# The opening of a transformer layer as one list of steps, with the order of ScalarE and VectorE fixed up to raw tile 25

## The chip, the core and the metric

The kernel runs on one core of a Trainium2 chip. TensorE (PE) multiplies and transposes, VectorE (DVE) and ScalarE (ACT) work element by element, GpSimd (POOL) does little here, and SyncE (SP) issues the loads from HBM to SBUF. Each engine works through its own queue in order. The metric is the time of one execution on the device in microseconds (us), less is better.

## The reference

One layer for 256 tokens of width 2048: a gated feed-forward block, a mixer of two attention branches, a second feed-forward block and a norm, each block conditioned on a vector c through nine vectors of modulation. The opening of the kernel computes the first lines of this:

```python
mod = (jax.nn.silu(c) @ w_ada[i] + b_ada[i]).reshape(B, N_MOD, D)
sh1, sc1, ga1, sh2, sc2, ga2, sh3, sc3, ga3 = [mod[:, j, None, :] for j in range(N_MOD)]
h = _rms_norm(x, g_ffn1[i]) * (1.0 + sc1) + sh1
x = x + 0.5 * ga1 * _swiglu(h, w1_a[i], w3_a[i], w2_a[i])
...
def _swiglu(h, w1, w3, w2):
    return (jax.nn.silu(h @ w1) * (h @ w3)) @ w2
```

All inputs are fp32. `w_ada` is 2048 by 18432, `w1_a` and `w3_a` are 2048 by 5632.

## The kernel before

Weights come in tiles of 128 partitions by 2048 fp32 numbers, 1 MiB each, called **raw tiles**. Almost all products are made in three passes (`mm3`): ScalarE casts half a raw tile at a time to the reduced type fp32r (`wh`, L125), VectorE subtracts to get the rest (`wl`, L126), and TensorE adds wh x hTh, wl x hTh and wh x hTl (L137, L140, L141). hTh and hTl are the two parts of the transposed, normed and modulated input h, by k-tile of 128 rows of the contraction.

The **opening** computes twelve results of the first feed-forward block (six chunks of 512 columns for `w1_a` and for `w3_a`), by 48 raw tiles of four weight blocks each. `opening_order` fixes which blocks a raw tile holds. The contraction runs in three groups of k-tiles: k-tile 0 alone (raw 0 to 2, in plain fp32, L630), k-tiles 1 to 5 (raw 3 to 17), k-tiles 6 to 15 (raw 18 to 47). A raw tile of the later groups is 24 products. Results that have ended in one group leave PSUM and are added up in SBUF (`add_up`): ScalarE copies the first part (L586), VectorE adds the later ones (L580).

A k-tile of h needs its modulation first, and that takes 32 **ada tiles**, two for each k-tile, numbered 0 to 31 here: VectorE multiplies each with silu(c) and sums along the row (L194). Then come two columns on ScalarE (`ab`, L528 and L530), hf (L542), hTh (two casts, L555) and hTl on VectorE (L562). x itself is scaled, transposed by TensorE and copied back in blocks of four k-tiles (L345, L348, L513).

Loads are all issued by SP, in the order of the program. A raw or ada tile takes a buffer from one of two pools, three buffers `raws` and a ring of seven shared with the sums in SBUF (`ramp_raw`); six sums leave one of the seven from raw 8 on. A load waits on SP until the last reader of its buffer has ended, and what is behind it waits too.

What sets the order before: the loop over raw tiles (`for r, grp in enumerate(raws_of)`, L656) loads ada tiles up to a target for each raw tile (`target`, L494), prepares h as soon as its ada tiles are known (`h_tiles`, `low_tiles`), splits the raw tile (`split_raw`) and records its products. TensorE's instructions of the first two groups and SP's loads are held in program order. Those of ScalarE and VectorE are placed by a scheduler, with a few hints (`issue_after`).

Of the kernel before, what the change touches and what calls it, by code (L numbers as in the profile page):

```python
# [63 lines left out]
def layer_kernel(ctx: ExitStack, tc: tile.TileContext, a: dict):
# [396 lines left out]
    with tc.tile_pool(name="f1", bufs=1, reuse_waits="tile") as f1, \  # L461
# [50 lines left out]
        def keep_x(tb, k0, ps):
            ACT.copy(x_sb[:, tb, k0 * P:(k0 + 4) * P], ps)  # L513
            for k in range(4):
                xnT.pop((k0 + k, tb))

        def h_tiles(known):

            while h_rows:
                k0, n = h_rows[0]  # L520
                if any((j, k) not in (known if n > 1 else ada_done) for j in range(2) for k in range(k0, k0 + n)):
                    return
                h_rows.pop(0)
                if k0 == 0:
                    mod_cols(0, 0, 1, C_GF1)
                for k in range(max(k0, 1), k0 + n):
                    with tc.issue_after(last_cast[0].ins) if n > 1 else nullcontext():
                        ACT.activation(ab[0][:, k:k + 1], mod[:, KT + k:KT + k + 1], AF.Identity,  # L528
                                       scale=cols[:, C_GF1 + k:C_GF1 + k + 1], bias=gbs[0][:, k:k + 1])
                        ACT.activation(ab[0][:, KT + k:KT + k + 1], mod[:, k:k + 1], AF.Identity,  # L530
                                       bias=cols[:, C_BADA + k:C_BADA + k + 1])
                hf = wkB("hf") if k0 else hl.tile([P, 1024], F32, tag="wh", name="hf")
                hf = hf[:, :TB * n * P].rearrange("p (t k n) -> p t k n", t=TB, k=n)
                for k in range(n):
                    scale, bias = ab[0][:, k0 + k:k0 + k + 1], ab[0][:, KT + k0 + k:KT + k0 + k + 1]
                    if (k0 + k, 0) in xnT:
                        for tb in range(TB):
                            with tc.issue_after(last_xn[0].ins):
                                first_hf[0] = ACT.activation(hf[:, tb, k], xnT[k0 + k, tb], AF.Identity, scale=scale, bias=bias)
                    else:  # L540
                        with tc.issue_after(last_cast[0].ins) if n > 1 else nullcontext():
                            ACT.activation(hf[:, :, k], x_sb[:, :, (k0 + k) * P:(k0 + k + 1) * P], AF.Identity,  # L542
                                           scale=scale, bias=bias)
                if k0 == 0:
                    gb = wk.tile([P, 16], F32, tag="gb", name="gb", bufs=1)
                    DVE.scalar_tensor_tensor(out=gb, in0=cols[:, C_BADA + KT:C_BADA + 2 * KT], scalar=1.0,
                                             in1=cols[:, C_GF1:C_GF1 + KT], op0=ALU.add, op1=ALU.mult)
                    gbs.append(gb)
# [891 lines left out]
```

## Time and profile before

| | |
|---|---|
| median of three runs | 2144.58 us (2140.0 to 2145.95) |
| the profiled execution | 2144.17 us |
| its span, first to last instruction | 2142.3 us |
| mean granted TensorE clock | 0.997 |
| loads over the span | 546.47 MB read, mean 256 GB/s |

The views used are: the page (busy time of each engine over the span); tables by window, in which each row is a stretch of the span with the busy us and number of instructions of each engine, the granted clock, the busy share of the DMA engines and GB/s; the waits, grouped by who waited for whom (total us, times, longest); and rows of the timeline (start us, duration us, engine, source line, operation, out<-in with shapes, number of instructions merged into the row, and in brackets the idle time before the row and what ended it).

### The profile page before, as it was taken

Reading aid. Unit: us, or ns where it says so; the run is one execution under the profiler, and the core shown is the slowest. Engines: PE = TensorE matmul, PEld = TensorE weight load, DVE = VectorE, ACT = ScalarE, POOL = GpSimd, SP = SyncE. Lnnn points to the kernel's source line nnn. Section 1 sums busy time; section 2 is a strip of 40 time slices with the busy share of each in tenths; the row PEclk is TensorE's granted clock in tenths of the full one; section 3 lists DMA queues with packets and bytes.
Section 4 is the critical chain, followed back from the end, with each engine's and each line's share of the span. In section 5 each row is a group of like instructions: output and inputs, shape, how many; then the busy total and the mean of one; then the engine's idle time right before and its main releaser. Section 6 shows DMA issues by size and latency. Waiting matters only on the chain.

```text
span 2142.3 us, 26049 instructions
## 1 busy us (share of the span) xinstructions
PE 2111.0 (99%) x10192; PEld 1757.9 (82%) x10192; DVE 1621.5 (76%) x1809; ACT 1045.5 (49%) x1320; POOL 41.7 (2%) x63
## 2 busy tenths in 40 slices
PE   8899999999999999999999999999999999999998
PEld 5677888888888879888877788778888888888886
DVE  5888667878777877565777778887688678857875
ACT  6546433343443465655544434475455445535553
POOL 0000000000000001010000000000000000000000
PEclk9999999999999999999999999999999999999999
DMA  9898668999988846445878788955555555555563
GB/s 394 325 372 329 241 237 325 352 338 337 351 332 306 324 153 210 163 165 198 301 289 302 277 332 302 338 204 194 202 194 191 205 177 196 215 197 196 178 216 118
DMA packets 79102, 550.30 MB, mean 257 GB/s; under 512 B 9409, under 2 KB 9969, under 8 KB 14082
## 3 DMA queue, kind: packets, MB, share of 16 engines
q1 hardware_dynamic: 76176, 542.06, 69.3%
q0 software_dynamic: 1344, 3.17, 0.5%
q10 hardware_dynamic: 1458, 3.40, 0.4%
q8 instruction: 80, 1.31, 0.2%
q14 instruction: 44, 0.36, 0.0%
HBM read 546.47 MB, written 2.12 MB: 256 GB/s over the span
## 4 chain that ended last, share of the span: by engine, by line
PE 85%; DVE 5%; DMA 5%; ACT 3%; issue 1%; POOL 0%; SPq 0%; POOLq 0%; ACTq 0%; DVEq 0%
PE a L137 9%; PE a L140 9%; PE a L141 9%; PE y L137 8%; PE y L140 8%; PE y L141 8%; PE pacc L140 3%; PE pacc L141 3%; PE pacc L137 3%; DVE wl L126 2%; DMA raw<-in_w_out 2%; ACT wh L125 2%; DVE raw L194 1%; DMA raw<-in_w_open 1%; PE qkv L137 1%
## 5 line engine op out<-in xcount | busy, mean ns | idle before, releaser
L125 ACT CAST wh<-raw 128x1024 fp32r<-128x1024 f32 (+2 forms) x678 | 690.9, 1040 | 860.4 <-DMA raw<-in_w_a 209.0
L126 DVE TENSOR_TENSOR wl<-raw,wh 128x1024 fp32r<-128x1024 f32 (+2 forms) x678 | 805.0, 1209 | 340.6 <-ACT wh L125 337.6
L194 DVE SCALAR_TENSOR_TENSOR raw<-raw,c_bc 128x2048 f32<-128x2048 f32 x144 | 329.2, 2287 | 26.8 <-DMA raw<-in_w_ada 25.7
L137 PE MATMUL a<-wh,hTh 128*128 128x512 f32 (+1 forms) x904 | 340.1, 376 | 0.1
L140 PE MATMUL a<-wl,hTh 128*128 128x512 f32 (+1 forms) x904 | 339.5, 376 | 0.0
L141 PE MATMUL a<-wh,hTl 128*128 128x512 f32 (+1 forms) x904 | 339.2, 375 | 0.0
L137 PE MATMUL y<-wh,gT 128*128 128x512 f32 x704 | 275.6, 391 | 0.2
L140 PE MATMUL y<-wl,gT 128*128 128x512 f32 x704 | 274.3, 390 | 0.0
L141 PE MATMUL y<-wh,gT 128*128 128x512 f32 x704 | 273.7, 389 | 0.0
L141 PEld LDWEIGHTS a<-wh,hTl 128*128 128x128 f32 x904 | 170.2, 188 | 31.0 <-DVE hTl L369 0.3
L137 PEld LDWEIGHTS a<-wh,hTh 128*128 128x128 f32 x904 | 170.3, 188 | 30.4 <-ACT wh L125 0.6
L140 PEld LDWEIGHTS a<-wl,hTh 128*128 128x128 f32 x904 | 170.3, 188 | 29.3
L137 PEld LDWEIGHTS y<-wh,gT 128*128 128x128 f32 x704 | 132.2, 188 | 29.6 <-ACT gT L392 1.8
L141 PEld LDWEIGHTS y<-wh,gT 128*128 128x128 f32 x704 | 132.1, 188 | 27.5
L140 PEld LDWEIGHTS y<-wl,gT 128*128 128x128 f32 x704 | 132.2, 188 | 27.0
L140 PE MATMUL pacc<-wl,hTh 128*128 128x512 f32 x360 | 141.9, 394 | 4.9 <-DVE wl L126 4.9
L137 PE MATMUL pacc<-wh,hTh 128*128 128x512 f32 x360 | 137.1, 394 | 7.2 <-ACT wh L125 6.3
L141 PE MATMUL pacc<-wh,hTl 128*128 128x512 f32 x360 | 140.6, 391 | 0.7 <-DVE hTl L562 0.7
L1272 DVE TENSOR_TENSOR wl<-right,wh 128x1024 fp32r<-128x1024 f32 x60 | 73.5, 1224 | 30.4 <-ACT wh L1271 29.9
L1271 ACT CAST wh<-right 128x1024 fp32r<-128x1024 f32 x60 | 63.2, 1053 | 56.0 <-PE m L141 24.8
L137 PEld LDWEIGHTS pacc<-wh,hTh 128*128 128x128 f32 x360 | 67.9, 189 | 24.0 <-ACT wh L125 8.4
L140 PEld LDWEIGHTS pacc<-wl,hTh 128*128 128x128 f32 x360 | 67.9, 189 | 21.8 <-DVE wl L126 8.1
(353 smaller groups left out, 3099.1 us busy)
## 6 DMA issues: line engine op xcount, KB each, us to landing
raw<-in_w_ada SPq DMA_DIRECT2D x144, 1024.0 KB, 5.9
raw<-in_w_b SPq DMA_DIRECT2D x102, 1024.0 KB, 4.8
raw<-in_w_a SPq DMA_DIRECT2D x84, 1024.0 KB, 5.5
raw<-in_w_in SPq DMA_DIRECT2D x60, 1024.0 KB, 5.0
raw<-in_w_open SPq DMA_DIRECT2D x45, 1024.0 KB, 6.3
raw<-in_w_s SPq DMA_DIRECT2D x30, 1024.0 KB, 4.8
raw<-in_w_out SPq DMA_DIRECT2D x16, 1024.0 KB, 6.4
raw<-in_w_proj_a SPq DMA_DIRECT2D x8, 1024.0 KB, 4.8
```

The costliest lines, as they stand in the source:

```text
L125: last_cast[0] = ACT.copy(wh[:, :w], src)
L126: DVE.tensor_tensor(wl[:, :w], src, wh[:, :w].bitcast(F32), op=ALU.subtract)
L137: m = PE.matmul(out, xh, wh, start=start, stop=False)
L140: PE.matmul(out, xh, wl, start=False, stop=False)
L141: PE.matmul(out, xl, wh, start=False, stop=stop)
L194: last_ada[0] = DVE.scalar_tensor_tensor(out=raw, in0=raw, scalar=1.0, in1=c_bc, op0=ALU.mult, op1=ALU.mult, accum_out=dst)
L1271: ACT.copy(wh[:, :n], src)
L1272: DVE.tensor_tensor(wl[:, :n], src, wh[:, :n].bitcast(F32), op=ALU.subtract)
```

## The change

The loop for raw tiles 0 to 25 is replaced by a list of steps, `opening_steps`, that a table of functions carries out one by one. Each letter is a step: A loads an ada tile, a multiplies it, R loads a raw tile, K and k make wh and wl of half of it, G makes the columns of a k-tile on ScalarE (g makes them on VectorE), H its hTh, h its hTl, F the first hf, X, T and Y scale, transpose and copy back a block of x, P records the products of one weight block, S opens a fourth accumulator, C and c move an ended sum on ScalarE or VectorE. Every instruction of these steps is held in program order (`pin`), on ScalarE and VectorE too. From raw tile 26 on the loop is as before. What is computed is the same; the columns of k-tiles 1 and 5 move from ScalarE to VectorE.

```diff
+BY_ROW = 26
...
+def opening_steps(order):
...
+    add("A A R0 A R1 A A R2 A R3")
+    add("Y F Y Y Y P0.0 X P0.1 T C H0.1 a h0.1 X C P0.2 T Y X P0.3 T C Y X")
+    add("P1.0 T C Y a g1.1 P1.1 C Y H1.1 a h1.1 S P1.2 C P1.3 C C P2.0 P2.1 P2.2 P2.3")
+    add("A R4 a K3.0 K3.1 k3.0 k3.1 G2.1 H2.1 P3.0 P3.1 P3.2 P3.3")
+    add("a h2.1 A A R5 K4.0 K4.1 k4.0 k4.1 a G3.1 H3.1 P4.0 P4.1 P4.2 P4.3")
+    add("A A R6 a h3.1 K5.0 K5.1 k5.0 k5.1 a G4.1 H4.1 P5.0 P5.1 P5.2 P5.3")
+    add("A R7 a K6.0 K6.1 k6.0 h4.1 k6.1 a g5.1 P6.0 P6.1 P6.2 P6.3")
+    add("R8 K7.0 H5.1 K7.1 k7.0 h5.1 k7.1 P7.0 P7.1 P7.2 P7.3")
+    loaded = done = 12
+    rows, low = list(range(6, KT, 2)), ""
+    for r in range(8, BY_ROW):
+        n = min(2 * KT, 12 + (20 * (r - 7) + 17) // 18) - loaded
+        add("A " * n + f"R{r + 1} K{r}.0 K{r}.1 k{r}.0 k{r}.1 {low} {ends(r - 1)}")
+        loaded += n
+        low = ""
+        if rows and 2 * rows[0] + 4 <= done:
+            add(f"G{rows[0]}.2 H{rows[0]}.2")
+            low = f"h{rows.pop(0)}.2"
+        add(f"P{r}.0 P{r}.1 P{r}.2 P{r}.3 " + "a " * (loaded - done))
+        done = loaded
+    add(low + " " + " ".join(f"G{k}.2 H{k}.2 h{k}.2" for k in rows))
+    return out
...
-        early = (2, 3, 5, 7, 8, 10, 11, 12)
-        marks = [(len(early) - 1, early[-1]), (25, n_ada), (len(raws_of), n_ada + ADA_END)]
...
+        def cast(r, q):
+            wh, wl = (hl.tile([P, 1024], F32R, tag=t, name=t) for t in ("wh", "wl"))
+            last_cast[0] = pin(ACT.copy(wh, raw_of[r][:, q * 1024:(q + 1) * 1024]))
+            part_of[r, q] = wh, wl
+
+        def cast_low(r, q):
+            wh, wl = part_of[r, q]
+            pin(DVE.tensor_tensor(wl, raw_of[r][:, q * 1024:(q + 1) * 1024], wh.bitcast(F32), op=ALU.subtract))
...
+        for s in script[2:]:
+            steps[s[0]](*s[1:])
...
-        for r, grp in enumerate(raws_of):
-            known = set(ada_done)
-            fill(int(target(r)) - (n_all - len(ada_q)))
...
+        for r in range(BY_ROW, len(raws_of)):
+            grp = raws_of[r]
```

Three places in the engines' queues. First SP, the loads behind raw 2. Names carry buffer numbers: before, raw_325, 374, 422 and 467 are raw 3 to 6; after, raw_228, 333, 381 and 426. Before:

```order
L665 DMA raw_301<-in_w_open 128x1024
L108 DMA raw_319<-in_w_ada 128x2048
L108 DMA raw_322<-in_w_ada 128x2048
L108 DMA raw_325<-in_w_open 128x2048
L108 DMA raw_371<-in_w_ada 128x2048
L108 DMA raw_374<-in_w_open 128x2048
L108 DMA raw_416<-in_w_ada 128x2048
L108 DMA raw_419<-in_w_ada 128x2048
L108 DMA raw_422<-in_w_open 128x2048
L108 DMA raw_464<-in_w_ada 128x2048
L108 DMA raw_467<-in_w_open 128x2048
```

After the change:

```order
L675 DMA raw_224<-in_w_open 128x1024
L150 DMA raw_226<-in_w_ada 128x2048
L150 DMA raw_228<-in_w_open 128x2048
L150 DMA raw_331<-in_w_ada 128x2048
L150 DMA raw_333<-in_w_open 128x2048
L150 DMA raw_377<-in_w_ada 128x2048
L150 DMA raw_379<-in_w_ada 128x2048
L150 DMA raw_381<-in_w_open 128x2048
L150 DMA raw_422<-in_w_ada 128x2048
L150 DMA raw_424<-in_w_ada 128x2048
L150 DMA raw_426<-in_w_open 128x2048
```

Raw 3, 4 and 5 have each moved ahead of one ada tile.

Second ScalarE, around the casts of raw 3 and raw 4 (wh from raw_325 and raw_374). Before:

```order
L528 ACTIVATE ab0_83<-mod_80,gb_216,small_77 128x1
L530 ACTIVATE ab0_83<-mod_80,small_77 128x1
L542 ACTIVATE hf_343<-x_sb_76,ab0_83 128x256
L555 CAST hTh_147<-hf_343 128x128
L555 CAST hTh_149<-hf_343 128x128
L528 ACTIVATE ab0_83<-mod_80,gb_216,small_77 128x1
L125 CAST wh_327<-raw_325 128x1024
L125 CAST wh_331<-raw_325 128x1024
L530 ACTIVATE ab0_83<-mod_80,small_77 128x1
L542 ACTIVATE hf_388<-x_sb_76,ab0_83 128x256
L125 CAST wh_376<-raw_374 128x1024
L125 CAST wh_380<-raw_374 128x1024
```

After, with raw_228 and raw_333:

```order
L607 COPY sum3_320<-pacc_95 128x1024
L680 CAST wh_336<-raw_228 128x1024
L680 CAST wh_339<-raw_228 128x1024
L565 ACTIVATE ab0_83<-mod_80,gb_164,small_77 128x1
L567 ACTIVATE ab0_83<-mod_80,small_77 128x1
L582 ACTIVATE hf_346<-x_sb_76,ab0_83 128x256
L586 CAST hTh_147<-hf_346 128x128
L586 CAST hTh_149<-hf_346 128x128
L680 CAST wh_383<-raw_333 128x1024
L680 CAST wh_386<-raw_333 128x1024
```

Before, columns and hf of k-tile 2 (hf_343) and the first column of k-tile 3 stand ahead of the casts of raw 3; after, the casts stand ahead of the columns and hf of k-tile 2 (hf_346).

Third SP again, later: raw_835, 875, 921 and 960 are raw 15 to 18 before, raw_806, 843, 889 and 930 after. Before:

```order
L108 DMA raw_835<-in_w_open 128x2048
L108 DMA raw_869<-in_w_ada 128x2048
L108 DMA raw_872<-in_w_ada 128x2048
L108 DMA raw_875<-in_w_open 128x2048
L108 DMA raw_918<-in_w_ada 128x2048
L108 DMA raw_921<-in_w_open 128x2048
L108 DMA raw_957<-in_w_ada 128x2048
L108 DMA raw_960<-in_w_open 128x2048
```

After:

```order
L150 DMA raw_806<-in_w_open 128x2048
L150 DMA raw_841<-in_w_ada 128x2048
L150 DMA raw_843<-in_w_open 128x2048
L150 DMA raw_887<-in_w_ada 128x2048
L150 DMA raw_889<-in_w_open 128x2048
L150 DMA raw_926<-in_w_ada 128x2048
L150 DMA raw_928<-in_w_ada 128x2048
L150 DMA raw_930<-in_w_open 128x2048
```

The two ada tiles in a row have moved from ahead of raw 16 to ahead of raw 18; the same goes for raw 25, which had two ahead of it and now has one.

More of the change, by code (lines that the diff above doesn't have):

```diff
@@ L60, in opening_order, with add, ends @@
     return [slots[q:q + 4] for q in range(0, len(slots), 4)]
+def opening_steps(order):
+    out = []
+    def add(text):
+        for t in text.split():
+            out.append((t[0],) + tuple(int(v) for v in t[1:].split(".") if v))
+    def ends(r):
+        return " ".join("c" if c < 4 else "C" for gi, c, wi, k in order[r]
+                        if gi == 1 and k == STARTS[2] - 1 and (c, wi) not in FRONT[2])
+    add("A A R0 A R1 A A R2 A R3")
[20 more added lines that the diff above has]
+    return out
 @with_exitstack
@@ L512, in keep_x @@
[L512 to L533, printed above, removed]
-                for k in range(n):
[L535 to L548, printed above, removed]
@@ new lines, in x_turn, with x_keep, ada_load @@
+                pin(PE.transpose(ps[:, k * P:(k + 1) * P], xn[:, k * P:(k + 1) * P], ident))
+            xbs.append((k0, tb, ps))
+            return ps
+        def x_keep():
+            k0, tb, ps = xbs.pop(0)
+            pin(ACT.copy(x_sb[:, tb, k0 * P:(k0 + 4) * P], ps))
+        ada_tiles = [(j, kt) for kt in range(KT) for j in (1, 0)]
+        ada_raws = []
+        def ada_load():
+            j, kt = ada_tiles.pop(0)
+            ada_raws.append((j, kt, load_unit(a["w_ada"][j, kt], pool=ramp_raw)))
@@ new lines, in ada_product, with columns @@
+        def ada_product():
+            j, kt, raw = ada_raws.pop(0)
+            ada_done.add((j, kt))
+            return pin(DVE.scalar_tensor_tensor(out=raw, in0=raw, scalar=1.0, in1=c_bc, op0=ALU.mult, op1=ALU.mult,
+                                                accum_out=mod[:, j * 16 + kt:j * 16 + kt + 1]))
+        def columns(k0, n):
+            for k in range(k0, k0 + n):
+                pin(ACT.activation(ab[0][:, k:k + 1], mod[:, KT + k:KT + k + 1], AF.Identity,
+                                   scale=cols[:, C_GF1 + k:C_GF1 + k + 1], bias=gb[:, k:k + 1]))
+                pin(ACT.activation(ab[0][:, KT + k:KT + k + 1], mod[:, k:k + 1], AF.Identity,
+                                   bias=cols[:, C_BADA + k:C_BADA + k + 1]))
@@ L566, in pieces, with low_parts @@
+        def low_parts(k0, n):
+            hf = hfs[k0] if k0 == 0 else hfs.pop(k0)
+            for tb in range(TB):
+                pin(DVE.tensor_tensor(hT[tb][1][:, k0:k0 + n, :], hf[:, tb],
+                                      hT[tb][0][:, k0:k0 + n, :].bitcast(F32), op=ALU.subtract))
         def pieces(acc):
@@ new lines, in layer_kernel @@
+        for s in script[2:]:
+            steps[s[0]](*s[1:])
+            if s[0] == "F":
+                pin(DVE.scalar_tensor_tensor(out=gb, in0=cols[:, C_BADA + KT:C_BADA + 2 * KT], scalar=1.0,
+                                             in1=cols[:, C_GF1:C_GF1 + KT], op0=ALU.add, op1=ALU.mult))
+        assert not (ada_tiles or ada_raws or xns or xbs or x_next or ended)
+        for r in range(BY_ROW, len(raws_of)):
+            grp = raws_of[r]
+            fill(ADA_END * (r - BY_ROW + 1) // (len(raws_of) - BY_ROW) - (n_all - len(ada_q)))
+            raw = raw_of.pop(r) if r in raw_of else load_unit(a["w_open"][r], pool=ramp_raw)
+            weights = split_raw(raw, 2048, 512)
+            do_todo(r)
+            for (gi, c, wi, k), w in zip(grp, weights):
```

202 lines of the change are left out of this document (103 added, 99 removed).

## The prediction

> **What bounds the kernel now.** I read the page first, then one table of windows by stage, then TensorE's waits, then single rows of the timeline.
>
> ```profile
> span 2142.3 us, 26049 instructions
> PE 2111.0 (99%) x10192; PEld 1757.9 (82%) x10192; DVE 1621.5 (76%) x1809; ACT 1045.5 (49%) x1320; POOL 41.7 (2%) x63
> ```
>
> The execution behind this page took 2144.17 us, 1.9 us more than its span and 0.4 us under the median of the three runs, 2144.58 us. TensorE is busy 99% of the span, so the change can only win what TensorE idles, and lose by making it idle. The windows say where that is (columns: length, then busy us of PE, PEld, DVE, ACT, POOL, then granted clock, DMA share, GB/s).
>
> ```profile
> 0.00:17.00 17.00, 13.06 (x76) 12.12 (x77) 8.63 (x20) 10.19 (x20) 1.16 (x7) 0.90 0.87 338
> 17.00:40.00 23.00, 23.00 (x70) 10.98 (x69) 11.94 (x13) 17.54 (x34) 0.00 (x0) 1.00 1.02 419
> 40.00:60.00 20.00, 14.99 (x55) 11.45 (x56) 15.16 (x19) 9.01 (x16) 0.00 (x0) 0.91 0.97 401
> 60.00:110.00 50.00, 46.31 (x198) 36.29 (x197) 43.00 (x45) 25.95 (x37) 0.00 (x0) 1.00 0.85 315
> 110.00:176.00 66.00, 63.54 (x278) 51.74 (x276) 58.13 (x56) 28.01 (x45) 0.00 (x0) 1.00 0.97 375
> 176.00:186.00 10.00, 8.29 (x34) 6.16 (x35) 7.32 (x8) 9.49 (x16) 0.00 (x0) 1.00 0.92 357
> 200.00:320.00 120.00, 120.00 (x556) 99.79 (x555) 86.08 (x84) 53.01 (x57) 1.28 (x2) 1.00 0.67 240
> ```
>
> TensorE is full from 17 to 40 us (raw tiles 0 to 2, in fp32) and from 200 us on. Between, it idles 5.01 + 3.69 + 2.46 + 1.71 = 12.9 us, and a clock of 0.91 over 20 us costs 1.8 us more. That stage, raw tiles 3 to 26, is what the change orders anew. Its waits, grouped, and the largest ones singly:
>
> ```profile
> PE pacc L137 <- ACT wh L125: 6.3, 4, 1.8
> PE pacc L140 <- DVE wl L126: 4.9, 7, 1.0
> PE pacc L137 <- ACT hTh L555: 0.9, 1, 0.9
> 41.70 0.51 PE L137 MATMUL pacc<-wh,hTh 128*128 128x512 f32 x1 [1.70 <-ACT wh L125]
> 57.32 0.49 PE L137 MATMUL pacc<-wh,hTh 128*128 128x512 f32 x1 [1.79 <-ACT wh L125]
> 100.83 0.50 PE L140 MATMUL pacc<-wl,hTh 128*128 128x512 f32 x1 [0.86 <-DVE wl L126]
> 125.11 0.50 PE L137 MATMUL pacc<-wh,hTh 128*128 128x512 f32 x1 [1.10 <-ACT wh L125]
> 126.37 0.50 PE L140 MATMUL pacc<-wl,hTh 128*128 128x512 f32 x1 [0.76 <-DVE wl L126]
> 177.11 0.73 PE L137 MATMUL pacc<-wh,hTh 128*128 128x512 f32 x2 [1.71 <-ACT wh L125]
> ```
>
> A raw tile is two casts (wh) and 24 products. Counting cast pairs, 41.70 is raw 3, 57.32 raw 5, 125.11 raw 16, 177.11 raw 25. From raw 16 to raw 25 are nine tiles in 52.0 us with waits of 0.76 and 1.71: 49.5 / 9 = **5.50 us a tile** when TensorE doesn't wait. Raw 2 ends at 41.70 - 1.70 = 40.0, so without any wait raw 25 would begin at 40.0 + 22 x 5.50 = 161.0. It begins at 177.1: **16.1 us are lost** by then, the idle time and the clock loss up to there (14.1) and about 2 us of pipeline that refills after each wait.
>
> **What each loss hangs on.** For raw 3 and 5:
>
> ```profile
> 35.37 0.50 DVE L562 TENSOR_TENSOR hTl<-hf,hTh 128x128 fp32r<-128x128 f32 x2 [4.42 <-ACT hTh L555]
> 35.78 2.29 DVE L194 SCALAR_TENSOR_TENSOR raw<-raw,c_bc 128x2048 f32<-128x2048 f32 x1
> 37.99 2.29 DVE L194 SCALAR_TENSOR_TENSOR raw<-raw,c_bc 128x2048 f32<-128x2048 f32 x1
> 38.44 0.60 ACT L542 ACTIVATE hf<-x_sb,ab 128x256 f32<-128x256 f32 x1
> 39.07 0.50 ACT L555 CAST hTh<-hf 128x128 fp32r<-128x128 f32 x2
> 40.32 0.39 ACT L528 ACTIVATE ab<-mod,gb,small 128x1 f32<-128x1 f32 x1 [0.75 <-DVE raw L194]
> 40.62 1.98 ACT L125 CAST wh<-raw 128x1024 fp32r<-128x1024 f32 x2
> 41.68 2.36 DVE L126 TENSOR_TENSOR wl<-raw,wh 128x1024 fp32r<-128x1024 f32 x2 [0.98 <-ACT wh L125]
> ```
>
> No DMA ends the wait at 40.62: raw 3 lay in SBUF, and ScalarE's queue held its cast behind a column (L528) that needs the seventh ada product, while VectorE had stood 4.42 us in front of a subtraction. In the changed kernel the casts of raw 3 (L680) stand ahead of the columns (L565), and raw 3 is loaded ahead of that seventh ada tile. For raw 16 and 25 it is a load:
>
> ```profile
> 111.52 2.60 SPq L108 DMA_DIRECT2D raw<-in_w_ada  x2
> 116.00 0.33 SPq L108 DMA_DIRECT2D raw<-in_w_open  x1
> 162.32 4.09 SPq L108 DMA_DIRECT2D raw<-in_w_ada  x2
> 168.29 14.02 SPq L108 DMA_DIRECT2D raw<-in_w_open  x5
> 176.01 1.99 ACT L125 CAST wh<-raw 128x1024 fp32r<-128x1024 f32 x2 [6.45 <-DMA raw<-in_w_open]
> ```
>
> Both times SP loads two ada tiles ahead of one raw tile. The new list has two in a row ahead of raw 5, 6, 9 and 18.
>
> **The new order, step by step.** Loads first. By the windows 5.75 MB (of 10^6 bytes) have landed at 17 us and 419 GB/s follow, 2.50 us a tile of 1.049 MB. In the new list raw 3 ends at 12.89 MB, so at 17 + 7.14 / 0.419 = 34.0; then ada 6, raw 4 at 39.0, two ada, raw 5 at 46.6, two ada (49.1, 51.6), raw 6 at 54.1, ada 11 at 56.6, raw 7 at 59.1; past 60 us I take the 375 GB/s of 110 to 176, 2.80 us a tile: raw 8 at 61.8, two ada, raw 9 at 70.2. What is seen landing is later:
>
> ```profile
> 24.97 2.29 DVE L194 SCALAR_TENSOR_TENSOR raw<-raw,c_bc 128x2048 f32<-128x2048 f32 x1 [2.35 <-DMA raw<-in_w_ada]
> 28.65 2.29 DVE L194 SCALAR_TENSOR_TENSOR raw<-raw,c_bc 128x2048 f32<-128x2048 f32 x1 [1.38 <-DMA raw<-in_w_ada]
> ```
>
> These are ada 3 and 4, due at 24.0 and 26.5 by the same count: 1.0 and 2.1 late. I add 1.5.
>
> - Start: the first hf stands one x copy earlier, worth 0.3 us; raw 3 can begin at 39.7.
> - Raw 3: cast from 35.5, second wl at 38.9, its k-tile ready by then: no wait, so 2.45 us of idle and the 1.8 us of slow clock go.
> - Raw 4: its casts follow hTh of k-tile 2 at 40.5, the second wl ends at 44.1; due 45.2. No wait.
> - Raw 5: ada 7 ends at 46.3, two columns, hf and two casts (0.7 + 0.60 + 0.50) make hTh at 48.0, then the casts; first wl 50.2, due 50.7. No wait, with 0.5 us to spare.
> - Raw 6: VectorE is now the chain. Ada 8 to 48.5, hTl, two wl to 51.3, ada 9 to 53.5, hTh at 55.2, ada 10 to 55.7, cast of raw 6 56.5, wl 57.7, hTl 58.2; due 56.2. It **waits 2.0**.
> - Raw 7: landing 60.6, ada 11 to 61.5, hTh 63.1, hTl 63.6: waits 0.3.
> - Raw 8 is ready early. Raw 8 to 13 have six pairs of wl at 2.28 (start to start; the rows' 2.36 and 2.29 overlap the next by 0.08), seven ada at 2.21, and, by the rows below, four sums at 1.2 and one hTl at 0.75: 13.7 + 15.5 + 4.8 + 0.75 = 34.7 us of VectorE against 33.0 of TensorE, with 1 us in hand: 0.6 remain. The sums (c) stand behind both wl of their tile, so that waits like the one at 100.83, which came of a sum that waited 0.92 for TensorE in front of a wl, go.
> ```profile
> 98.42 1.23 DVE L580 TENSOR_TENSOR sum<-pacc,sum 128x1024 f32<-128x1024 f32 x1 [0.92 <-PE pacc L141]
> 104.04 0.76 DVE L562 TENSOR_TENSOR hTl<-hf,hTh 128x256 fp32r<-128x256 f32 x2
> ```
>
> - Raw 18: two tiles a row take 5.60 us of DMA and 5.50 of TensorE, so raw 15 has about 1 us in hand, raw 18 nearly none of the 2.8 us of its extra ada: 2.4 remain.
> - Raw 19 to 25: 2.28 + 2.21 + 0.35 = 4.84 us of VectorE a tile, under 5.50: nothing added.
>
> Sum: 39.7 + 121.0 + 2.0 + 0.3 + 0.6 + 2.4 = **166.0** for raw 25, 11.1 us before 177.1. Check by bytes: 62.2 MB up to raw 25, 23.8 MB at 60 us, the rest at 375 GB/s ends at 162.4, plus 1.5 landing and 2.1 (cast, wl): 166.0. Raw 26 needs columns 14 and 15 from the last ada tile, with about 0.7 us of waits as before.
>
> Later the row from 200 to 320 shows TensorE at 120.00 of 120.00 and DMA at 0.67: work that arrives 11 us earlier runs 11 us earlier. **2144.17 - 11.1 = 2133.1 us.** ScalarE's steps cost nothing: it is busy 28.01 of 66 us in the last long window. If its cover goes, a cast of 0.95 stands before each product of a tile. The unknowns are the lag of a landing (1.0 to 2.1 seen: raw 6 and 7 move by no more than 0.6), the DMA rate past 60 us (419 gives all but raw 6 back: 161.0 + 2; 357 below), and whether the waits removed also carry the refill: from 16.1 + 0.3 won, 2127.8, down to nothing.
>
> A second gap of clock: where TensorE waited at 41.70 and 42.96 the clock fell to half; after the like waits at 57.32 it did not.
>
> ```profile
> 45.00:46.00 1.00, 1.00 (x4) 0.50 1.04 434
> 59.00:60.00 1.00, 1.00 (x6) 1.00 0.20 82
> ```
>
> So raw 6's 2.0 us may or may not cost 1.8 us again; I take nothing, since the nearest row with products of this kind on both sides is 57.32. The Trainium skill, TensorE: Matmul & The Clock Gate, Part 1, says the clock is halved after an idle window of about 3.4 us that runs freely. The trace disagrees at 40 us, where a gap of 1.70 and one of 0.75 sufficed; by the page's figure neither gap would have cost clock and the sum would hold, by the row it may lose 1.8.
>
> **Rivals.**
>
> - **The loads stay slower.** For it: 375 GB/s at a share of 0.97, against 419 at 1.02 earlier, and 357 in the last window. At 357 from 60 us on, raw 25 lands at 60 + 38.4 / 0.357 = 167.6, starts at 171.2, and 5.9 us are won: 2138.3. Against it: 401 and 419 held for 43 us in this very trace. The Trainium skill, DMA: Bandwidth & Descriptors, Specifications, gives about 358 GB/s as a core's HBM limit; the 419 of this trace is over it, so it is no hard bound here.
> - **The queue still runs dry**, the list not doing what it says. From 60 to 110 the DMA share was 0.85, because SP waited in order for a raw buffer. The buffers are as few as before. If that share comes back for 50 us, 8 us go and raw 25 starts at 174 with the lag: won 3, 2141.
> - **Given back later**: a load-bound stage behind that waits at the same time whatever comes ahead. Against it: 120.00 of 120.00 in that row. 2144.
> - **Slower.** Past raw 8 four raw buffers turn. A load in the trace takes 7.4 us from issue to landing (raw 21: issued 143.34, cast 150.65), then 3.4 for cast and wl, 10.8 a turn of two tiles, 5.4 each. If the fixed order makes VectorE stand before a wl while a landed ada tile waits behind it, a turn grows by 2.29 to 13.1, 6.55 a tile: 17 tiles x 1.05 = 18 us, less 9 won earlier, 2153. It decides from the point where wl reaches VectorE before its cast by more than about 1.1 us in every tile.
>
> ```profile
> 143.34 0.33 SPq L108 DMA_DIRECT2D raw<-in_w_open  x1
> 150.65 2.00 ACT L125 CAST wh<-raw 128x1024 fp32r<-128x1024 f32 x2 [3.00 <-DMA raw<-in_w_open]
> ```
>
> **How the numbers follow.** Chances: my forecast 0.57 (2128 to 2137), slower loads 0.16, a dry queue 0.12, given back 0.06, slower 0.09. The likeliest gives 2133.1. The range runs from everything won, 2127, to 2142, which leaves out the slower case, the one given back and a little below. 0.3%, 6.4 us or 2137.7, is about what a measurement of this kernel can tell from no change: faster 0.57 plus a third of the loads' case and some of the next, 0.64; slower 0.09; within 0.27.
>
> **What would show it.** Right: raw 3's first product directly behind raw 2 at about 39.7 with the clock at 1.0 there; the largest waits at raw 6 (about 58) and raw 18 (about 124); raw 25 begun near 166; a DMA share above 0.95 from 60 to 110. Wrong: waits of ScalarE's casts on TensorE or on VectorE in raw 3 to 8, SP issues more than 7 us apart there, raw tiles 9 to 25 above 5.6 us each, or new idle time past 200 us.

## The result and the profile after

| | before | after |
|---|---|---|
| median of five runs (lowest to highest) | 2144.58 us (2140.0 to 2145.95) | 2132.02 us (2131.82 to 2133.57) |
| span of the profiled execution | 2142.3 us | 2130.2 us |
| ratio after / before, 95% interval | | 0.9946 [0.9932, 0.9961] |

The kernel became faster by 12.6 us by the medians and 12.1 us by the spans; 2133.1 had been forecast. The table of windows of the changed kernel, columns as before:

```profile
17.00:40.00 23.00, 23.00 (x72) 11.53 (x71) 13.24 (x18) 19.10 (x35) 0.00 (x0) 0.99 1.02 419
40.00:60.00 20.00, 18.78 (x81) 14.83 (x80) 18.93 (x23) 9.36 (x16) 0.00 (x0) 1.00 1.01 417
60.00:110.00 50.00, 49.64 (x218) 40.52 (x217) 47.61 (x50) 27.85 (x43) 0.00 (x0) 1.00 0.97 376
110.00:176.00 66.00, 63.42 (x275) 50.91 (x274) 56.15 (x57) 32.95 (x50) 0.00 (x0) 1.00 0.94 365
176.00:186.00 10.00, 10.00 (x46) 8.26 (x45) 10.00 (x12) 5.07 (x5) 0.00 (x0) 1.00 0.85 336
200.00:320.00 120.00, 120.00 (x549) 99.56 (x548) 89.35 (x90) 53.08 (x58) 1.28 (x2) 1.00 0.71 256
```

TensorE's idle time from 40 to 186 us is 1.22 + 0.36 + 2.58 + 0 = 4.2 us, where it was 12.9: 8.7 less. The clock between 40 and 60 us is 1.00 where it was 0.91: 1.8 less. The other 1.6 of the 12.1 us are a remainder, which would fit refills of TensorE's pipeline behind the waits that went; no run shows them apart. From 200 to 320 us TensorE is full, as it was, so no wait came back there.

TensorE's waits of the changed kernel from 38 to 200 us, from the timeline, with the two rows at which raw 3 and raw 25 begin:

```profile
39.80 0.79 PE L179 MATMUL pacc<-wh,hTh 128*128 128x512 f32 x1
57.20 0.50 PE L179 MATMUL pacc<-wh,hTh 128*128 128x512 f32 x1 [0.47 <-ACT wh L680]
58.45 0.50 PE L182 MATMUL pacc<-wl,hTh 128*128 128x512 f32 x1 [0.76 <-DVE wl L685]
97.21 0.50 PE L182 MATMUL pacc<-wl,hTh 128*128 128x512 f32 x1 [0.36 <-DVE wl L685]
126.08 1.68 PE L179 MATMUL pacc<-wh,hTh 128*128 128x512 f32 x6 [1.16 <-ACT wh L680]
164.44 1.52 PE L179 MATMUL pacc<-wh,hTh 128*128 128x512 f32 x6
171.31 0.80 PE L179 MATMUL pacc<-wh,hTh 128*128 128x512 f32 x2 [1.27 <-ACT hTh L586]
```

Counting cast pairs again, 57.20 and 58.45 are raw 6, 97.21 raw 13, 126.08 raw 18, 171.31 raw 26. Raw 3, 5, 16 and 25, where the large waits stood, begin without one. Raw 25 begins at 164.4, 12.7 us earlier than 177.1.

### The profile page after: what moved, and what is told of

The parts are those of the page before. It is cut to its first block, busy times and chain, and to the rows that moved or that the text cites. A ratio compares the mean times of both kernels' runs of the same rounds, so it can differ in the third digit from the quotient of the medians.

```text
span 2130.2 us, 26048 instructions
## 1 busy us (share of the span) xinstructions
PE 2108.0 (99%) x10192; PEld 1757.7 (83%) x10192; DVE 1622.1 (76%) x1816; ACT 1043.5 (49%) x1316; POOL 41.7 (2%) x63
## 4 chain that ended last, share of the span: by engine, by line
PE 79%; DMA 10%; DVE 6%; ACT 3%; issue 2%; SPq 0%; POOL 0%; ACTq 0%; POOLq 0%; DVEq 0%
PE a L179 9%; PE a L182 9%; PE a L183 9%; PE y L182 6%; PE y L179 6%; PE y L183 6%; DMA raw<-in_w_open 4%; DMA raw<-in_w_ada 2%; DMA raw<-in_w_a 2%; DMA raw<-in_w_out 2%; DVE wl L168 2%; PE pacc L182 2%; PE pacc L183 2%; PE pacc L179 2%; PE qkv L179 1%
## 5 line engine op out<-in xcount | busy, mean ns | idle before, releaser
L167 ACT CAST wh<-raw 128x1024 fp32r<-128x1024 f32 (+2 forms) x632 | 644.3, 1039 | 813.2 <-DMA raw<-in_w_a 222.4
L168 DVE TENSOR_TENSOR wl<-raw,wh 128x1024 fp32r<-128x1024 f32 (+2 forms) x632 | 750.4, 1207 | 326.5 <-ACT wh L167 324.1
L236 DVE SCALAR_TENSOR_TENSOR raw<-raw,c_bc 128x2048 f32<-128x2048 f32 x112 | 256.1, 2287 | 16.9 <-DMA raw<-in_w_ada 16.3
```

Of the source, the lines that this page charges most:

```text
L167: last_cast[0] = ACT.copy(wh[:, :w], src)
L168: DVE.tensor_tensor(wl[:, :w], src, wh[:, :w].bitcast(F32), op=ALU.subtract)
L236: last_ada[0] = DVE.scalar_tensor_tensor(out=raw, in0=raw, scalar=1.0, in1=c_bc, op0=ALU.mult, op1=ALU.mult, accum_out=dst)
```

## The experiments

The change does three things at once: it orders the loads anew (the rival that the **loads** carry the gain), it fixes the **order of ScalarE's and VectorE's queues** (theory Q), and it puts casts ahead of columns on ScalarE in particular (theory C, a narrower Q). It also moves the columns of k-tiles 1 and 5 to VectorE, which no run tried apart. A second question is what paces raw tiles 6 to 26 now: bytes of the loads (theory D) or the turn of their buffers by way of VectorE (theory V, formed when D fell). Every run is compared with runs of the kernel before on the same chip. Its medians differ by up to 3.1 us between the chips, so it is the ratios that are compared, with 0.9946 [0.9932, 0.9961] of the changed kernel; a span from another chip stands only beside them.

| run | what it is | median us | before on that chip | ratio, 95% interval |
|---|---|---|---|---|
| e1_loads | before, new load list | 2144.66 | 2142.63 | 1.001 [0.9996, 1.0024] |
| e2_oldloads | after, old load list | 2133.25 | 2142.63 | 0.9958 [0.9943, 0.9973] |
| e3_free | after, ScalarE and VectorE not held in order | 2153.25 | 2142.63 | 1.0054 [1.0037, 1.0071] |
| e6_columns_first | after, columns ahead of casts | 2147.06 | 2143.15 | 1.002 [1.001, 1.0029] |
| e9_hint | before, one hint more | 2137.48 | 2143.15 | 0.9975 [0.9965, 0.9984] |
| e13_hint_loads | before, hint and new load list | 2139.39 | 2141.52 | 0.9987 [0.9978, 0.9996] |
| e4_more_r2 | after, 4.3 us more of TensorE at raw 2 | 2129.65 | 2142.63 | 0.9943 [0.9928, 0.9958] |
| e5_more_r33 | after, 4.3 us more of TensorE at raw 33 | 2134.29 | 2143.15 | 0.9963 [0.9952, 0.9975] |
| e7_half_ada | after, 20 ada tiles loaded by half | 2134.85 | 2143.15 | 0.9962 [0.9952, 0.9972] |
| e10_half_product | after, 20 ada tiles multiplied by half | 2127.51 | 2141.52 | 0.9934 [0.992, 0.9947] |
| e11_half_both | after, both halved | 2130.57 | 2141.52 | 0.9946 [0.9934, 0.9958] |
| e12_sums_first | after, sums ahead of wl | 2131.39 | 2141.52 | 0.9951 [0.9939, 0.9964] |

### Loads or queues: e1_loads, e2_oldloads, e3_free

The kernel before with the changed kernel's list of loads, everything else as it was:

```diff
-        early = (2, 3, 5, 7, 8, 10, 11, 12)
+        early = (2, 3, 5, 6, 7, 9, 11, 12)
...
+            if r < 26:
+                return 12 + (20 * (r - 8) + 17) // 18
...
-            h_tiles(known)
+            h_tiles(ada_done if r == 26 else known)
```

> The kernel before with the load list of the changed kernel alone: as many ada tiles ahead of each raw tile as in the new list, ScalarE and VectorE left to the scheduler. Theory L (the order of the loads carries the gain): raw 25 begins before 168 us and the time is 2135 us or less, since the waits at raw 3, 16 and 25 hung on a load or on an ada product one place too early. Theory Q (the fixed order of ScalarE's and VectorE's queues carries it): raw 25 begins after 171 us and the time is 2138 us or more, with waits at raw 5 to 7 and at the sums behind as before.

The changed kernel with the old list of loads (two of the places where the list changes):

```diff
-    add("A A R0 A R1 A A R2 A R3")
+    add("A A R0 A R1 A A R2 A A R3")
...
-        n = min(2 * KT, 12 + (20 * (r - 7) + 17) // 18) - loaded
+        n = min(2 * KT, 12 + 20 * (r - 6) // 18) - loaded
...
```

> The changed kernel with the load list of before: one ada tile more ahead of raw 3, 4, 5, 8, 16, 17 and 25 (so two in a row ahead of raw 16 and 25, and one ahead of raw 18), the fixed order of ScalarE and VectorE kept but for the place of two ada products. Theory L: 2138 us or more, with waits of 1.5 us and more at raw 3, 16 and 25. Theory Q: 2136 us or less, a wait under 1 us at raw 3, since its load lands 2.5 us later but its cast is no longer held by a column.

The changed kernel with TensorE's and SP's order as it is, but ScalarE's and VectorE's instructions left to the scheduler (one of the places; the others are alike):

```diff
-            last_cast[0] = pin(ACT.copy(wh, raw_of[r][:, q * 1024:(q + 1) * 1024]))
+            last_cast[0] = free(ACT.copy(wh, raw_of[r][:, q * 1024:(q + 1) * 1024]))
...
```

> The changed kernel with the same list of steps, but with ScalarE's and VectorE's instructions not held in program order (the scheduler places them; TensorE and SP are held as before). If holding the order is what wins (theory Q): 2137 us or more, with casts or sums placed early in front of something that waits. If the load list wins (theory L): 2131 to 2135 us.

The load list alone wins nothing (1.001). Its trace says why: the waits at raw 16 and raw 25 do go (TensorE idles 0.07 us from 110 to 176 us, where it idled 2.46), but waits of 1.40 and 0.76 come up at raw 6 and of 2.13 at raw 26. Without the list the fixed order keeps its gain: 0.9958 against 0.9946, intervals that overlap almost wholly, and TensorE's waits up to 200 us add up to 4.0 us in both. Without the fixed order the kernel is 0.5% slower than before, for two reasons. One is a wait of its own at 32 us, since the scheduler puts a step of k-tile 1 on ScalarE ahead of the copies of sums, for which TensorE waits (its waits, grouped: total us, times, longest); the clock is at 0.50 from 28 to 38 us there:

```profile
PE pacc L656 <- ACT sum L608: 7.7, 1, 7.7
```

The other is columns ahead of casts again, from raw 9 on. So the gain lies in the order of the queues, by the first two runs; the third has a wait of its own in it and can't be used as a price. Rows of ScalarE's timeline in the kernel with the new loads alone show what is still wrong there:

```profile
53.84 0.39 ACT L530 ACTIVATE ab<-mod,gb,small 128x1 f32<-128x1 f32 x1 [0.75 <-DVE raw L194]
54.13 1.98 ACT L125 CAST wh<-raw 128x1024 fp32r<-128x1024 f32 x2
59.80 0.29 ACT L532 ACTIVATE ab<-mod,small 128x1 f32<-128x1 f32 x1 [3.68 <-DVE raw L194]
```

The cast doesn't wait for its load: it follows the column at once. It stands behind a column that waits for an ada product, as in the kernel before.

### The place of the columns: e6_columns_first, e9_hint, e13_hint_loads

The changed kernel, fully held in order, with only the columns moved: each column stands where its ada product was made, ahead of the casts that follow (u is one column, G's work taken apart).

```diff
-    add("A R4 a K3.0 K3.1 k3.0 k3.1 G2.1 H2.1 P3.0 P3.1 P3.2 P3.3")
+    add("A R4 a u2.1 u2.0 K3.0 K3.1 k3.0 k3.1 H2.1 P3.0 P3.1 P3.2 P3.3")
...
-        add(f"P{r}.0 P{r}.1 P{r}.2 P{r}.3 " + "a " * (loaded - done))
+        add(f"P{r}.0 P{r}.1 P{r}.2 P{r}.3 " + "".join(f"a u{n // 2}.{1 - n % 2} " for n in range(done, loaded)))
...
```

> The changed kernel, all held in order as there, with one move on ScalarE alone: each column that needs an ada product stands ahead of the casts that follow that product's place in the list, instead of behind them (k-tiles 2, 3, 4 ahead of the casts of raw 3, 4, 5; k-tiles 6 to 15 likewise). VectorE's order and the loads are those of the changed kernel. Theory C (the place of columns and casts on ScalarE carries the gain and, past raw tile 8, the loss of the kernel with free queues): VectorE then stands about 1 to 2 us in front of a wl in each of raw 3 to 5 and in the rows past 8, 6.0 us a tile, 2145 to 2153. Rival: the order on VectorE or the place of the sums carries it: below 2135.

The reverse in the kernel before: the hint that its later k-tiles have (issue behind the last cast) is given to k-tiles 2 to 5 too, at the columns as shown and in the same words at hf.

```diff
-                    with tc.issue_after(last_cast[0].ins) if n > 1 else nullcontext():
+                    with tc.issue_after(last_cast[0].ins) if n > 1 or k0 > 1 else nullcontext():
...
```

> The kernel before with one hint more: columns and hf of k-tiles 2 to 5 too are issued behind the casts of the last raw tile, as those of the later k-tiles are already. On ScalarE the casts of raw 3, 4, 5 and so on then stand ahead of the columns; VectorE's order follows in a few places; SP's and TensorE's queues are the same as before. Theory C: the waits at raw 3 and raw 5 (41.70, 42.96, 57.32) go, 4 to 8 us are won up to raw 9, and raw 16 and 25 stay as they are: 2134 to 2140. Rival (the load list is needed for that): within 2 us of 2144.

The same with the changed kernel's list of loads on top (the edits of e1_loads and of e9_hint together):

> The kernel before with both the hint (columns and hf of k-tiles 2 to 5 behind the casts) and the changed kernel's list of loads. The hint alone gave ratio 0.9975, the loads alone 1.001. If the loads help only once ScalarE's order is mended, as the prediction's terms for raw 3, 16 and 25 have it: most of the gain, 2133 to 2135, ratio 0.995 to 0.996. If the loads are worth nothing either way and the rest lies in VectorE's order: as the hint alone, 0.997 to 0.998.

Moving the columns alone takes the whole gain away and a little more: 1.002. But it does not undo the gain where that was made, as its windows show (columns as in the table after the change):

```profile
40.00:80.00 40.00, 38.18 (x162) 29.84 (x161) 35.78 (x41) 20.67 (x33) 0.00 (x0) 1.00 0.95 382
80.00:200.00 120.00, 108.36 (x449) 82.05 (x448) 95.83 (x97) 54.70 (x80) 0.00 (x0) 1.00 0.89 325
```

Up to 80 us TensorE idles 1.8 us, hardly more than in the changed kernel (1.2) and far less than before (6.8). Past 80 us it idles 11.6, where the changed kernel idles 2.9 and the kernel before 6.0. For the k-tiles prepared there the kernel before already had its columns behind the casts, by its hint. So this run shows what columns ahead of casts cost in this kernel; that the gain at raw 3 to 5 came from their place rests on the run with the hint alone. The waits of VectorE for the casts, grouped (total us, times, longest) from 40 to 186 us, first in the kernel with the columns first, then in the changed kernel:

```profile
DVE wl L693 <- ACT wh L688: 25.9, 21, 1.5
```

```profile
DVE wl L685 <- ACT wh L680: 10.0, 14, 1.3
```

One period of the kernel with the columns first, in rows of ScalarE's and VectorE's timelines:

```profile
80.42 0.39 ACT L572 ACTIVATE ab<-mod,gb,small 128x1 f32<-128x1 f32 x1 [3.69 <-DVE raw L560]
80.71 1.98 ACT L688 CAST wh<-raw 128x1024 fp32r<-128x1024 f32 x2
78.09 2.28 DVE L560 SCALAR_TENSOR_TENSOR raw<-raw,c_bc 128x2048 f32<-128x2048 f32 x1
81.77 2.36 DVE L693 TENSOR_TENSOR wl<-raw,wh 128x1024 fp32r<-128x1024 f32 x2 [1.39 <-ACT wh L688]
84.05 1.28 DVE L620 TENSOR_TENSOR sum<-pacc,sum 128x512 f32<-128x512 f32 x2
85.25 2.28 DVE L560 SCALAR_TENSOR_TENSOR raw<-raw,c_bc 128x2048 f32<-128x2048 f32 x1
```

The ada product runs from 78.09 to 80.4; only then the column, then one cast, then wl at 81.77, the sum, and the next product at 85.25. Next to nothing overlaps in that ring: 85.25 - 78.09 = 7.16 us for this tile, which has a sum, where TensorE needs 5.50. VectorE idles 1.39 of it, waiting for a cast whose raw tile lies ready.

The hint wins 5.4 us of 2143.15, nearly half of the gain, with one condition and the old loads. The load list on top doesn't add to it (0.9987, if anything it takes some away). Of what is missing to the changed kernel, 1.89 and 0.53 us are waits at raw 25, whose cast waits for its load as before; with the list on top these go, and one of 3.43 comes up at raw 26. Another part lies on VectorE, as rows of the kernel with the hint show (ScalarE, then VectorE, then TensorE):

```profile
64.46 0.50 ACT L555 CAST hTh<-hf 128x128 fp32r<-128x128 f32 x2
64.68 2.28 DVE L194 SCALAR_TENSOR_TENSOR raw<-raw,c_bc 128x2048 f32<-128x2048 f32 x1
66.89 0.49 DVE L562 TENSOR_TENSOR hTl<-hf,hTh 128x128 fp32r<-128x128 f32 x2
67.23 0.50 PE L141 MATMUL pacc<-wh,hTl 128*128 128x512 f32 x1 [1.69 <-DVE hTl L562]
```

hTh was there at 64.96, but the subtraction that TensorE needed stood behind an ada product until 66.89. This is k-tile 5, whose h the list of steps puts ahead of the next ada product. VectorE's order matters at raw 3 too. The kernel before, and the one with the hint, let VectorE stand 4.42 and 4.26 us in front of hTl of k-tile 1, so that the next ada product begins at 35.8. In the changed kernel, which has the columns of k-tile 1 on VectorE itself, the two rows are:

```profile
30.31 0.49 DVE L591 TENSOR_TENSOR hTl<-hf,hTh 128x128 fp32r<-128x128 f32 x2 [0.54 <-ACT hTh L586]
32.35 2.29 DVE L560 SCALAR_TENSOR_TENSOR raw<-raw,c_bc 128x2048 f32<-128x2048 f32 x1 [1.55 <-DMA raw<-in_w_ada]
```

That product is 3.4 us earlier, which would explain why columns ahead of the casts cost so little before 80 us in the kernel with the columns first. How much each of VectorE's places is worth, the move of the columns of k-tiles 1 and 5 among them, was not tried apart.

### What paces raw tiles 6 to 26 now: e4_more_r2, e5_more_r33, e7_half_ada, e10_half_product, e11_half_both

Products repeated, so that TensorE has 4.3 us more to do by the estimate, once at raw 2 (raw 3 then begins at 43.57, 3.8 us later than in the changed kernel) and once at raw 33:

```diff
                 if gi == 0:
+                    if r == 2 and (tb == 0 or e == (4, 0)):
+                        pin(PE.matmul(out, hfs[k][:, tb, 0], weights, start=True, stop=True))
```

> The changed kernel with five of raw 2's fp32 products made twice (the first of each pair is overwritten): 5 x 0.86 = 4.3 us more of TensorE work ahead of raw 3, nothing else. Theory S (waits add up, each us of TensorE in the opening shows in the time): 4.3 us over the changed kernel, about 2136. Theory D (the landing of the loads paces raw 6 to 26): the waits at raw 6, 18 and 26, some 7 us in all with the refill behind them, shrink by most of the 4.3, and the time rises by 1.5 us or less, to 2133.5 at most.

```diff
                 else:
+                    if first and r == 33:
+                        for _ in range(10 - tb):
+                            PE.matmul(out, xs(k, tb)[0], weights[0], start=True, stop=True)
```

> The changed kernel, with 19 more fp32 products (4.3 us of TensorE at 0.227 us each) at raw tile 33, past the stage that the change orders anew; each repeats a product that the next one overwrites, so the result is the same. It is the counterpart of the 4.3 us added at raw tile 2. If TensorE sets the end there: 2132.0 + 4.3 = 2136.3, ratio 0.9966 to before. If the loads still pace the kernel past raw tile 26, these 4.3 us cost nothing either: 2132, ratio 0.995.

At raw 33 the work costs about what it takes: 0.9963 against 0.9946 is 3.6 us, and in the trace raw 26 begins at 171.18, as without it (171.31), but the span is 4.0 us longer, 2134.2. At raw 2 it costs nothing: 0.9943, and raw 26 begins at 170.18. The intervals of the three ratios overlap or nearly touch, so the reading rests on the traces as much as on the times. TensorE's waits of the kernel with more work at raw 2 from 80 to 200 us, and none before:

```profile
125.96 1.68 PE L179 MATMUL pacc<-wh,hTh 128*128 128x512 f32 x6 [0.19 <-ACT wh L682]
170.18 0.80 PE L179 MATMUL pacc<-wh,hTh 128*128 128x512 f32 x2 [0.38 <-ACT hTh L586]
171.13 0.73 PE L182 MATMUL pacc<-wl,hTh 128*128 128x512 f32 x2 [0.15 <-DVE wl L168]
```

Raw 18 begins at 125.96 where it was 126.08, and the waits up to 200 us fall from 4.0 to 0.7 us: more work at raw 2 only fills waits that were due. So something other than TensorE sets raw 18 and raw 26. Theory D takes it to be bytes; the next run halves those of 20 ada tiles and leaves VectorE its time, by making the half product twice:

```diff
-            ada_raws.append((j, kt, load_unit(a["w_ada"][j, kt], pool=ramp_raw)))
+            half = kt >= 6
+            ada_raws.append((j, kt, load_unit(a["w_ada"][j, kt][:, :1024] if half else a["w_ada"][j, kt],
+                                              1024 if half else 2048, pool=ramp_raw)))
...
+                for _ in range(2):
...
```

> The changed kernel with the 20 ada tiles of k-tiles 6 to 15 loaded by half (0.5 MiB less each, 10.5 MB in all); their product is made twice over the half that is loaded, so VectorE does as much as before, and the second half of these ada products is left out of the result. Theory D (landing of the loads paces raw tiles 6 to 26): the waits at raw 6 and later go, as far as they are the loads', 3 to 4 us less than the changed kernel, 2128 to 2129. Rival (VectorE or the queues set these waits): 2132, no change.

Nothing is won, and raw 18 still waits (1.14 and 0.76 us), although the DMA share from 60 to 110 us fell from 0.97 to 0.80. **Theory D falls.** (The total is blurred on two sides: two half products take 2.41 us together where one whole takes 2.21, and the clock was 0.97 from 110 to 176 us, some 2 us. The wait at raw 18 stands ahead of that clock loss.) Rows of VectorE, of SP (the load of raw 18 is issued) and of ScalarE (it is cast), for the changed kernel and then for the one with half the bytes:

```profile
115.57 2.29 DVE L560 SCALAR_TENSOR_TENSOR raw<-raw,c_bc 128x2048 f32<-128x2048 f32 x1
117.90 0.33 SPq L150 DMA_DIRECT2D raw<-in_w_open  x1
124.98 1.99 ACT L680 CAST wh<-raw 128x1024 fp32r<-128x1024 f32 x2 [6.00 <-PE pacc L183]
```

```profile
117.93 1.23 DVE L564 SCALAR_TENSOR_TENSOR raw<-raw,c_bc 128x1024 f32<-128x1024 f32 x1
119.20 0.33 SPq L150 DMA_DIRECT2D raw<-in_w_open  x1
126.09 1.99 ACT L688 CAST wh<-raw 128x1024 fp32r<-128x1024 f32 x2 [6.89 <-PE pacc L183]
```

Each time SP issues the load 0.04 us after an ada product has ended (115.57 + 2.29 = 117.86; 117.93 + 1.23 = 119.16), as a load would that waited for the buffer of that ada tile, and the cast follows 7.1 and 6.9 us later, with the ada loads ahead of it whole or halved. (Both rows name TensorE as the releaser, whose last product of raw 17 ended at the same moment; in the kernels with more work at raw 2 and with half products the same cast names the load, 7.2 and 7.9 us after its issue. With more work at raw 33, a kernel equal to the changed one up to there, it names the load too, 8.0 us after its issue, when TensorE had stood still for 0.9 us.) If that ring paces the stage, theory V, then less VectorE helps where fewer bytes didn't:

```diff
+            if kt >= 6:
+                return pin(DVE.scalar_tensor_tensor(out=raw[:, :1024], in0=raw[:, :1024], scalar=1.0, in1=c_bc[:, :1024],
+                                                    op0=ALU.mult, op1=ALU.mult,
+                                                    accum_out=mod[:, j * 16 + kt:j * 16 + kt + 1]))
```

> The changed kernel, loads as there, but VectorE multiplies only the first half of the 20 ada tiles of k-tiles 6 to 15 (1.22 us each in place of 2.29, 21 us less of VectorE in all); the other half of these ada products is left out of the result. Theory V (halving the bytes won nothing, so what paces raw tiles 9 to 26 is the turn of the raw buffers: VectorE's product frees a buffer, SP then issues the next load, 7 us later it lands): the buffer behind raw 18 is freed 1 to 2 us earlier, the waits at raw 10 and raw 18 (0.36, 1.16) go, 1 to 3 us less than the changed kernel, ratio 0.993 to 0.994. Rival (bytes after all, or only the time of one load): ratio 0.9946 to 0.996 as before.

And both halves left out, loads and products:

> The changed kernel with both halves left out for the 20 ada tiles of k-tiles 6 to 15: half the bytes loaded and one product over that half. Theory V: nothing past the kernel that halves the products alone, ratio 0.993 to 0.994, waits at raw 5 and 6 only, and up to 2 us of them. If bytes and VectorE bind by turns: 1 to 2 us less again. If neither: ratio 0.9946 to 0.996, with a wait at raw 18 as before.

The same three rows with the product halved:

```profile
112.36 1.22 DVE L561 SCALAR_TENSOR_TENSOR raw<-raw,c_bc 128x1024 f32<-128x1024 f32 x1
113.62 0.33 SPq L150 DMA_DIRECT2D raw<-in_w_open  x1
121.50 2.00 ACT L684 CAST wh<-raw 128x1024 fp32r<-128x1024 f32 x2 [5.63 <-DMA raw<-in_w_open]
```

The load of raw 18 goes out 4.3 us earlier, and from 60 to 186 us TensorE doesn't wait at all. The ratio is 0.9934 against 0.9946 for the changed kernel; these two intervals overlap, but the kernel with all of VectorE's work and half the bytes (0.9962 [0.9952, 0.9972]) lies clear of it. With both halves left out the waits at raw 13, 18 and 26 are gone as well, as theory V has it, but the time misses what V expected (0.993 to 0.994): 0.9946, no better than the changed kernel. Its profiled execution is the fastest of five, 2127.91 us; the other four, 2130.46 to 2132.12, have no profile, so the cause stays open. In that profile TensorE waits at 196.57 (0.81 us for gT on VectorE), where it was full in the changed kernel. So the waits bear theory V out: less work on VectorE takes them away, fewer bytes don't. In time the stake is about 2.6 us by the two ratios, which is not clear of noise. Nor do the runs part the turn of the buffers from a VectorE that is simply full: in the table after the change it is busy 47.61 of 50 us from 60 to 110, and half products lighten its queue and free the buffers at once. What the rows of the load show is the way by which it reaches TensorE at raw 18.

### Where the sums stand: e12_sums_first

```diff
-        add("A " * n + f"R{r + 1} K{r}.0 K{r}.1 k{r}.0 k{r}.1 {low} {ends(r - 1)}")
+        add("A " * n + f"R{r + 1} K{r}.0 K{r}.1 {ends(r - 1)} k{r}.0 k{r}.1 {low}")
```

> The changed kernel with the sums of raw tiles 9 to 14 on VectorE (steps c) ahead of both wl of their row, where the kernel before had some of them, instead of behind; everything else stays in its order. The prediction's view: a sum waits up to 0.9 us for TensorE in front of a wl, so waits of 0.9 to 1.0 come back at raw 9 to 14, 1 to 3 us in all by the trace, and ratio 0.995 to 0.996. Rival (a sum in front costs nothing, since wl waits for its cast there anyway): no wait above 0.5 at raw 9 to 14, ratio as the changed kernel's.

Rows of VectorE and TensorE around raw 12 and raw 13 of that kernel:

```profile
90.07 1.23 DVE L612 TENSOR_TENSOR sum<-pacc,sum 128x1024 f32<-128x1024 f32 x1 [1.01 <-PE pacc L183]
92.48 0.50 PE L182 MATMUL pacc<-wl,hTh 128*128 128x512 f32 x1 [0.86 <-DVE wl L685]
98.07 1.23 DVE L612 TENSOR_TENSOR sum<-pacc,sum 128x1024 f32<-128x1024 f32 x1 [1.63 <-PE pacc L183]
100.48 0.50 PE L182 MATMUL pacc<-wl,hTh 128*128 128x512 f32 x1 [2.23 <-DVE wl L685]
```

The waits come back, 3.09 us of them at raw 12 and 13, by the mechanism that the prediction named. The time hardly moves: 0.9951 against 0.9946, although the interval alone would leave room for the 3 us. The trace is clearer: raw 18's wait falls from 1.16 to 0.25 and raw 26's from 1.27 to none ahead of its first product, so that raw 18 begins 2.0 us later than in the changed kernel, but raw 26 only 0.4 (171.73 against 171.31). Waits of TensorE at raw 12 and 13 mostly take the place of those that were due at raw 18 and 26.

## Why the prediction was right, step by step

- **Start, 39.7, and raw 3 to 5 without a wait**: held. Raw 3 began at 39.80, and raw 5 came in time. The reason too: the cast of raw 3 waited for its load and no longer for a column. But the earlier load of raw 3, 4 and 5, which the prediction put beside it, was not needed (e2_oldloads, e13_hint_loads).
- **Raw 6, a wait of 2.0**: 1.23. The prediction called VectorE the chain there. Rows of ScalarE and VectorE say otherwise:

```profile
56.09 1.99 ACT L680 CAST wh<-raw 128x1024 fp32r<-128x1024 f32 x2 [0.33 <-DMA raw<-in_w_open]
57.17 1.23 DVE L685 TENSOR_TENSOR wl<-raw,wh 128x1024 fp32r<-128x1024 f32 x1 [0.69 <-ACT wh L680]
```

  The last to come was the landing of raw 6, 2.0 us after its 54.1 by cumulated bytes, inside the lag seen before; VectorE stood idle 0.69 us for the cast. ScalarE had been free for only 0.33 us when the load came, so the two chains ended close together, and a wait of about the right size came by luck, for the wrong reason.
- **Raw 7, 0.3; raw 9 to 14, 0.6**: none, and 0.36 at raw 13. (The prediction's own figures, 34.7 - 33.0 - 1, give 0.7 for the second.) Putting the sums behind wl does remove their waits, but by e12_sums_first this was worth 0.4 us at raw 26.
- **Raw 16 and 25, whose waits were to go with the two ada tiles ahead of them**: no wait at either. The old list with the fixed order (e2_oldloads) leaves 0.76 us at raw 16 and 0.53 at raw 25, and none at raw 18, so by these figures the place of those two tiles moves a wait more than it makes one.
- **Raw 18, 2.4, by bytes of two ada tiles in a row**: 1.16, and bytes are not the reason. This is the step that failed: "two tiles a row take 5.60 us of DMA and 5.50 of TensorE" took the loads for a stream at a rate. e7_half_ada halves the stream and leaves the wait; e10_half_product frees the buffer earlier and the wait goes. The prediction had the right ring in its list, in the rival on four turning buffers (7.4 us from issue to landing; its rows give 7.3), and didn't use it for raw 18.
- **The sum**: 39.8 + 121.0 + 1.23 + 0.36 + 1.16 = 163.6 against 164.4 measured; 0.9 us are left, which would fit refills; the prediction had not counted any behind the waits that stay. Raw 25 began 1.6 us earlier than forecast.
- **Raw 26, about 0.7 as before**: 1.27, since its k-tile's second column waits for the last ada product; and the kernel before had no such wait there, its raw 26 begins at 183.72 without one. Three rows of ScalarE of the changed kernel:

```profile
168.74 0.29 ACT L567 ACTIVATE ab<-mod,small 128x1 f32<-128x1 f32 x1 [2.94 <-DVE raw L560]
169.92 1.03 ACT L167 CAST wh<-raw 128x1024 fp32r<-128x1024 f32 x1
170.86 0.71 ACT L586 CAST hTh<-hf 128x256 fp32r<-128x256 f32 x2
```

  So 12.4 of the 12.7 us are left at raw 26, and 12.1 reach the end, nearly 1:1 as forecast. That the forecast time, 2133.1, missed by only 1.1 us owes something to luck: the waits of raw 6, 7, 9 to 14 and 18 were put 2.6 us too high, and the refills behind them and raw 26 too low.
- **DMA from 60 us on, 375 GB/s at a share over 0.95**: 376 at 0.97, then 365 at 0.94. The queue did not run dry. The rivals of slower loads and of a dry queue didn't come.
- **Clock, no loss at raw 6**: 1.00 from 40 to 60 us.
- **The slower rival**, priced at 6.55 us a tile and 2153: half of its mechanism is real. With columns ahead of the casts VectorE stands 1.39 us in front of wl, more than the 1.1 given as the point from which it decides, at 7.16 us for a tile with a sum; the kernel came out at 2147. But no cast of it waits for a load from 64 to 190 us, so the ring there runs through ScalarE's queue and not, as the rival had it, through the buffers. The kernel with free queues, at 2153, has 7.7 us from elsewhere in it. The list doesn't do it, because casts lead there.
- **What each part was worth**, which the prediction had left together: casts ahead of the columns of k-tiles 2 to 5, 5 us in the kernel before; the load list, nothing that these runs can tell; the rest, some 4 to 6 us (0.9975 to 0.9958 with the old loads, to 0.9946 with the new), by the rows in good part the order on VectorE and what follows from it, but no run tried that order by itself. These parts need not add up: each kernel's waits hide others.

## What to carry to other kernels

An instruction that waits holds everything behind it in its engine's queue: look in the timeline for a short one (here a column of 0.3 us) that stands ahead of a cast whose load has landed, and move it behind, before ordering loads anew. When undoing a move makes the kernel slow again, look where the new waits stand: they may be others than those that the move took away. Do not add up an engine's waits as if each were worth its length: give that engine a few us more work ahead of them, and see whether the end moves. And where loads turn through few buffers, ask what frees the buffer; here that, plus the time of one load, ended the wait at raw 18, while half of the ada bytes made no difference.
